# One hybrid decoder layer: heads interleaved with their up-projections, small work one tile later, the output halves reordered

## The chip, the core and the metric

The kernel runs on one core of a Trainium2 chip. The metric is the device time of one execution in microseconds (us); of several runs the median counts. Before the change three runs took 1225.09, 1226.62 and 1227.04 us: median 1226.62.

The engines are TensorE (PE in the profile; its weight loads are PEld), VectorE (DVE), ScalarE (ACT), GpSimd (POOL) and SyncE (SP), which here only issues DMAs. Each engine runs its own instructions strictly in the order of the program; between engines, semaphores hold an instruction back until its operands are there.

## What is computed

One decoder layer on 256 tokens of width 2048, in float32. One input projection feeds two groups of heads: an RWKV-7 mixer (16 heads of 64, a recurrence over the tokens) and a latent attention (8 heads of 128, with a rotary part). Both outputs are joined and projected back, and then comes a gated MLP with a short convolution. Cut to what matters here:

```python
h = rms_norm(x, attn_norm_g)
proj = h @ w_in                                  # 2048 x 4512
shifted = token_shift(proj[..., :RWKV_SHIFT_DIM], rwkv_mu)
h_r, h_k, h_v, h_w, h_a, h_g = _split(shifted, IN_SPLITS[:6])
c_q, c_kv, k_pe = _split(proj[..., RWKV_SHIFT_DIM:], IN_SPLITS[6:])
# rwkv7_mixer: per token  sa = state @ a_t
#   state = state * w_t + sa b_t + v_t k_t ;  y_t = state @ r_t
# then group norm, bonus, gate:  y = (gn(y) + bonus) * g
y_rwkv = rwkv7_mixer(h_r, h_k, h_v, h_w, h_a, h_g, ...)
# mla_mixer: q = rms_norm(c_q) @ w_uq ; k, v = rms_norm(c_kv) @ w_ukv
#   p = softmax(causal(q_nope k_nope + rope(q_pe) rope(k_pe))) ; out = p v
y_mla = mla_mixer(c_q, c_kv, k_pe, positions, ...)
x = x + concatenate([y_rwkv, y_mla]) @ w_out
x = x + conv_glu_ffn(rms_norm(x, ffn_norm_g), ...)
return rms_norm(x, final_norm_g)
```

## The kernel before, in words

**Products.** Weights come in pieces of 128x1024 floats (512 KB). `piece` (L123 to L130) loads one into `raw`, ScalarE makes the rounded half `hi`, VectorE the rest `lo = raw - hi`; three buffers each. `prod_b` (L156 for hi, L159 for lo) multiplies pieces with the stacked hi and lo halves of the activations into a PSUM tile `mm`; `prod_a` (L176 to L178) does the same with weights as the moving side. There are three `mm` buffers. `joined` (ScalarE L164, VectorE L165 and L166) reads the two halves of such a tile, adds and scales them; only then is its buffer free.

**Input tiles.** `in_tile(i)` does one tile of 128 columns of the input projection from two pieces. Small work that hangs behind a tile is put into a list, `pend`, and run by `flush`, which stands between the two pieces of the next `in_tile`. In this list are the key norms, the chunk products `gram`, the bonus and the solve.

**The solve.** The recurrence is done in four chunks of 64 tokens. `gram` makes each chunk's matrices `G` and stores their diagonal blocks to `dL` in device memory (16 stores). `solve` loads them as `Lp`, one row per system (L556), multiplies by the scales `Mp` on VectorE (L560), and runs 31 elimination steps on VectorE (`tm` L564, `Tq` L566). The inverse goes back by memory, is completed on TensorE (`pR` L609, `pT` L622), and stands in `TT`.

**The recurrence.** `chunk(c)` works in two halves of the heads. For each: `px` from the state `ST` and `UV`; VectorE makes `XB` (L669); `px` again from `XB` and `TT`; `UV` is copied by VectorE and ScalarE (L675); `pS` and `py` follow from `UV`, and VectorE updates `ST` (L688, L689). All TensorE rows of it carry L658, and all its PSUM tiles come from a pool `ch` of three.

**Attention.** `latent` makes the two normalized latents `cl`. `up_b` makes the up-projections: `wuq` tiles into `qn`, `wuk` tiles into `kn`, two tiles for each of two heads to a side, four times. `wuv` makes `vm`. For each head `scores(h)` fills `psc` (pool `at` of two) and does the softmax in `pexp` on VectorE and ScalarE; `attend(h)` transposes it (`ptp`), multiplies by `vm` (`po`) and writes `yhi[1]` and `ylo[1]`. `group_norm(w)` normalizes the recurrence's output `yt[w]` on VectorE (L700 to L722), multiplies by the gate (`pgate`), transposes (`pyT`), and writes `yhi[0]` and `ylo[0]`.

**Output.** `w_out` is done in two halves of its rows (half 0 takes the recurrence's output, half 1 that of attention) and four blocks of columns; `x1` collects the sums.

**What sets the order.** The program text gives priorities; a scheduler then fixes each engine's order of instructions when the kernel is built. So a block that is written earlier can still run late, and the order on each engine is what counts.

Of the kernel before, what the change touches and what calls it, by code (L numbers as in the profile page):

```python
# [54 lines left out]
def hybrid_layer(ctx: ExitStack, tc: tile.TileContext, a: dict, out: bass.AP):  # L55
    nc = tc.nc
# [15 lines left out]
    def s4(dt=F32, n="s4"):  # L72
        return sb.tile([P, 1024], dt, tag="s4", name=nm(n), bufs=NS4)

    def sv(n):
        return sb.tile([P, 1024], F32, tag="sv", name=nm(n), bufs=3)
# [67 lines left out]
    last_w, last_lo = [None], [None]  # L144
    pend = []

    def flush():
        while pend:
            pend.pop(0)()

# [29 lines left out]
    def in_tile(i, pf=mm):  # L182
        acc = pf()
        for h in range(2):
            prod_b(acc, piece(a["win"][i, h]), x_hl, h * 8, 8, h == 0, h == 1)
            if h == 0:
                flush()
        return acc

    def rsqrt(src, scale, eps, w, eng=None, part=None):  # L190
# [118 lines left out]
    with tc.manual_schedule(engines={mybir.EngineType.SP}):  # L309
        for g in range(4):  # L310
            xsplit(g)
            if g == 0:
                nc.scalar.dma_start(cst, a["cst"])
            if g == 2:
                rope_tables()
            if g % 2 == 0:
                for i in range(2):
                    pcs[i, g // 2] = piece(a["win"][wt0[i], g // 2])
            for i in range(2):
                hl = tuple(u[:, (g % 2) * 512:(g % 2 + 1) * 512] for u in pcs[i, g // 2])  # L320
                prod_b(acc0[i], hl, x_hl, g * 4, 4, g == 0, g == 3)
        for h in range(2):
            prod_b(acc0[2], piece(a["win"][26, h]), x_hl, h * 8, 8, h == 0, h == 1)
        sums(0)
        kacc[0] = in_tile(1)
        dve0 = last_lo[0]
        sums(1)
        kacc[1] = in_tile(2, ch)
        lora = s4(n="lora")
        nc.sync.dma_start(lora, a["lora"])  # L330

# [102 lines left out]
    for p in range(8):  # L434
        pp, g = p // 2, p % 2
        for q in range(4):
            if DP[q] == p:
                decay(q)
        acc = kacc[p] if p in kacc else in_tile(1 + p)
        k = shifted(acc, 1 + p)  # L440
        kc = k.rearrange("p (c t) -> p c t", t=64)
        sq = t1("ksq")
        S.activation(sq, k, AF.Square, scale=vv("kk", p))

        def key_ss(p=p, sq=sq):
            for w in range(2):
                PE.matmul(ssP[:, w * 16 + p * 2:w * 16 + p * 2 + 2], sq[:, w * P:(w + 1) * P], blk2,
                          start=True, stop=True)

        pend.append(key_ss)  # L450
        V.scalar_tensor_tensor(AR[pp][:, g, :, 0, 1:64], kc[:, :, 1:64], nkk[:, p:p + 1],
                               AR[pp][:, g, :, 1, 0:63], ALU.mult, ALU.mult)
        V.tensor_scalar(AR[pp][:, g, :, 0, 0:1], kc[:, :, 0:1], nkk[:, p:p + 1], None, ALU.mult)
        V.tensor_tensor(kv_(pp, g), kc, kv_(pp, g), ALU.mult)
        V.scalar_tensor_tensor(bv_(pp, g), kc, hkk[:, p:p + 1], bv_(pp, g), ALU.mult, ALU.mult)
# [17 lines left out]
        for pb in range(4):  # L473
            V.tensor_copy(Mp[pb * 32:(pb + 1) * 32, :], pmt[0:32, pb * 32:(pb + 1) * 32])

    pend.append(key_norms)


    BKt = []
# [1 line left out]
    dL = dr.tile([P, 32, 32], F32, name="dL")  # L481
# [3 lines left out]
    for p in range(8):  # L485
        pp, g = p // 2, p % 2
        acc = in_tile(9 + p)
        if p == 0:
            pend.append(key_norms_p)
        r = shifted(acc, 9 + p)  # L490
        rc = r.rearrange("p (c t) -> p c t", t=64)
        V.tensor_tensor(AR[pp][:, g, :, 1, :], rc, AR[pp][:, g, :, 1, :], ALU.mult)
        pr = t1("pr")
        V.tensor_tensor(pr.rearrange("p (c t) -> p c t", c=4), kv_(pp, g), AR[pp][:, g, :, 1, :], ALU.mult)

        def bonus(p=p, pr=pr):
            for w in range(2):
                PE.matmul(boP[:, w * 16 + p * 2:w * 16 + p * 2 + 2], pr[:, w * P:(w + 1) * P], brk[:, p, :],
                          start=True, stop=True)

        def gram(p=p, pp=pp):
            hf = p // 4
            e0 = (pp % 2) * 2
            for c in range(4):
                if pp % 2 == 0:
                    G1[c].append(s4(n="G1").rearrange("p (e t) -> p e t", e=8))
            for w in range(2):
                pg = [ch("pg") for _ in range(2)]
                for r in range(2):
                    for gg in range(2):  # L510
                        o = (r * 2 + gg) * P
                        for h in range(2):
                            hs = slice(h * 64, h * 64 + 64)
                            PE.matmul(pg[h][:, o:o + P], BK[pp][hs, gg, w * 2 + r, :, :],  # L514
                                      AR[pp][hs, gg, w * 2 + r, :, :], start=o == 0, stop=True,
                                      skip_group_check=True)
                for h in range(2):
                    for r in range(2):
                        V.tensor_tensor(G1[w * 2 + r][hf][:, h * 4 + e0:h * 4 + e0 + 2, :],
                                        pg[h][:, r * T:(r + 1) * T].rearrange("p (q t) -> p q t", q=2),  # L520
                                        gmask.unsqueeze(1).broadcast_to([P, 2, P]), ALU.mult)
            if pp % 2 == 1:
                for c in range(4):
                    for b in range(2):
                        r0 = 64 + b * 32
                        for h in range(2):
                            nc.sync.dma_start(dLv[b, c, :, h, hf * 4:hf * 4 + 4, :],
                                              G1[c][hf][r0:r0 + 32, h * 4:h * 4 + 4, b * 32:(b + 1) * 32])
            for c in range(3):
                if pp == 0:  # L530
                    BKt.append(s4(n="BKt").rearrange("p (a t) -> p a t", a=8))
                pt = ch("pt")
                for gg in range(2):
                    PE.transpose(pt[:, gg * P:(gg + 1) * P],
                                 BK[pp][:, gg, c, :, :].rearrange("p s t -> p (s t)"), ident)
                S.copy(BKt[c][:, pp * 2:pp * 2 + 2, :], pt[:, 0:T].rearrange("p (a t) -> p a t", a=2))

        pend.append(bonus)
        if g == 1:
            pend.append(gram)  # L540

    def bonus_rows():
        for r in range(2):
            V.tensor_copy(bon[:, r * 32:r * 32 + 32], boP[r * 64:r * 64 + 64, 0:32])

    pend.append(bonus_rows)


    TT = con([P, 32, 64], "TT")
    T11 = []  # L550

    def solve():
        Lp = sv("Lp").rearrange("p (i t) -> p i t", i=32)
        Tq = sv("Tq").rearrange("p (s t) -> p s t", s=32)
        tm = t1("tm")
        nc.sync.dma_start(Lp, dL)  # L556
        nc.gpsimd.memset(Tq, 0.0)
        nc.gpsimd.memset(Tq.rearrange("p s t -> p (s t)")[:, 0:1024:33], 1.0)
        nc.gpsimd.memset(TT, 0.0)
# [1 line left out]
        for i in range(31):  # L561
            n, m = i + 1, 31 - i
# [17 lines left out]
                k0 = h * 64 + b * 32  # L580
                nc.sync.dma_start(TT[k0:k0 + 32, :, b * 32:(b + 1) * 32], dT[k0:k0 + 32].rearrange("q s t -> s q t"))

    pend.append(solve)


    UV = [s4(n="UV").rearrange("p (e t) -> p e t", e=8) for _ in range(4)]
# [179 lines left out]

    latent(0, "qg", SC)
    latent(1, "kvg", 1.0)
    flush()
    qr = s4(n="qr").rearrange("p (h t) -> p h t", h=4)  # L770
    qs = sv("qs").rearrange("p (h t) -> p h t", h=4)
    qn, kn = a8("qn", F32), a8("kn", F32)
# [5 lines left out]
    def up_b(src, i, x, dsts):  # L778
        pcs = piece(src[i])
        for j in range(2):  # L780
            acc = mm()
            prod_b(acc, (pcs[0][:, j * 512:(j + 1) * 512], pcs[1][:, j * 512:(j + 1) * 512]),
                   lambda k: cl[x][k // 2][:, k % 2, :, :], 0, 4, True, True)
            joined(dsts[j], acc, rrB[x])
# [5 lines left out]
    V.tensor_tensor(qr, qr, cosR.unsqueeze(1).broadcast_to([P, 4, T]), ALU.mult)  # L790
    V.tensor_tensor(qs, qs, sinR.unsqueeze(1).broadcast_to([P, 4, T]), ALU.mult)
    V.tensor_tensor(qr, qr, qs, ALU.add)
    for i in range(4):
        up_b(a["wuq"], i, 0, [qn[:, i * 2 + j, :] for j in range(2)])
    for i in range(4):
        up_b(a["wuk"], i, 1, [kn[:, i * 2 + j, :] for j in range(2)])
    g2a = s4(n="g2a")
    g2b = s4(n="g2b")
    gnwb = [s4(n=n) for n in ("gnw", "gnb")]
# [5 lines left out]
    yhi = [[s4(F32R, "yhi").rearrange("p (k t) -> p k t", k=4) for _ in range(2)], a8("yhi")]  # L805
    ylo = [[s4(F32R, "ylo").rearrange("p (k t) -> p k t", k=4) for _ in range(2)], a8("ylo")]

    group_norm(0)
    for cc in range(2):
        accs = [mm() for _ in range(2)]  # L810
        for i in range(2):
# [2 lines left out]
                   i * 2, 2, i == 0, i == 1)  # L814
        for tb in range(2):
            S.activation(vm[tb][:, cc * 512:(cc + 1) * 512], accs[tb], AF.Copy, scale=rrs[1][:, tb:tb + 1])

    group_norm(1)

    soft = {}  # L820

# [33 lines left out]
        S.copy(yhi[1][:, h, :], po)  # L855
        V.tensor_tensor(ylo[1][:, h, :], po, yhi[1][:, h, :].bitcast(F32), ALU.subtract)

    for h in range(8):
        scores(h)
        if h > 0:  # L860
            attend(h - 1)
    attend(7)


# [7 lines left out]

    ssf = st("ssf", 8)
    zs = [hl4("z") for _ in range(4)]
    for half in (0, 1):
        for c in range(4):
            accs = [mm() for _ in range(2)]
            for i in range(4):
                if half == 0 and i == 2:
                    load_x1(c)  # L880
                prod_a(accs, piece(a["wout"][half, c, i]), lambda k: y_hl(yhi, half, k),
                       lambda k: y_hl(ylo, half, k), i * 2, 2, i == 0, i == 3)
            for tb in range(2):
                V.tensor_tensor(x1[c][:, tb, :], x1[c][:, tb, :], accs[tb], ALU.add)
            if half == 1:
                for tb in range(2):
                    scr = sb.tile([P, 512], F32, tag="xs", name=nm("scr"), bufs=2)
                    S.activation(scr, x1[c][:, tb, :], AF.Square, accum_out=ssf[:, tb * 4 + c:tb * 4 + c + 1])
# [39 lines left out]
    for blk, nf in enumerate((24, 20)):  # L928
        hh = [s4(F32R, "hh").rearrange("p (k t) -> p k t", k=4) for _ in range(nf // 4)]
        hl = [s4(F32R, "hl").rearrange("p (k t) -> p k t", k=4) for _ in range(nf // 4)]  # L930
        for fi in range(nf):
            f = f0 + fi
# [133 lines left out]
```

## Time and profile before

| | |
|---|---|
| median of three runs | 1226.62 us |
| the profiled execution | 1224.32 us |
| its span from first to last instruction | 1222.5 us |
| TensorE busy | 1186.5 us, 97% |
| VectorE busy | 837.9 us, 69% |
| ScalarE busy | 599.7 us, 49% |
| granted TensorE clock, mean | 0.986 |
| stages: input tiles, recurrence, heads, output, MLP | the MLP begins near 487 us and runs to the end |

In the rows that follow, a row of the timeline is: start, length, engine, line, operation, output <- inputs, shapes, count, and in brackets the idle time ahead of it on that engine with what ended it. A row of a group ends with busy us, mean ns of one | idle before. A row of waits is: who waited <- for whom: us in all, how often, the longest.

### The profile page before, as it was taken

The page shows a single profiled execution, that of the slowest core. Times are in us where ns is not written, and L with a number is a line of the kernel's source. Part 1 is how long each engine was busy: PE and PEld are TensorE (multiplying, and loading weights), DVE is VectorE, ACT ScalarE, POOL GpSimd, SP SyncE. Part 2 cuts the span into 40 slices and gives each one's busy share as a digit, 9 for nine tenths or more (in the row PEclk, how much of TensorE's full clock was granted, in tenths as well). Part 3 has the DMA queues.
Part 4 walks back from the last instruction along what each step waited for, and adds up shares of the span by engine and source line. Part 5 has one row for each costly group of instructions (what it writes and reads, how often), then busy time and mean ns, then how long its engine had stood idle before and what let it go on. Part 6 is the DMA issues. An engine that isn't in the chain of part 4 may idle for free.

```text
span 1222.5 us, 18434 instructions
## 1 busy us (share of the span) xinstructions
PE 1186.5 (97%) x6993; PEld 1001.6 (82%) x6993; DVE 837.9 (69%) x1359; ACT 599.7 (49%) x939; POOL 60.4 (5%) x202
## 2 busy tenths in 40 slices
PE   7989979999989999999999999999999999999996
PEld 5878868888847888888888888888888888888885
DVE  6898659868985656777777676454577777766563
ACT  6684425635334455555555554333455555554442
POOL 3400100002120001000000000000000000000000
PEclk9989999999999999999999999999999999999998
DMA  8735544744513555655555555666655555566662
GB/s 298 207 116 157 145 147 135 204 141 143 166 64 104 177 174 172 201 188 181 186 187 190 189 185 179 195 190 194 203 182 188 189 186 185 183 223 205 208 209 85
DMA packets 71017, 215.82 MB, mean 177 GB/s; under 512 B 17616, under 2 KB 17872, under 8 KB 70928
## 3 DMA queue, kind: packets, MB, share of 16 engines
q1 hardware_dynamic: 69776, 211.84, 53.9%
q10 hardware_dynamic: 768, 2.05, 0.6%
q8 instruction: 55, 0.90, 0.3%
q0 software_dynamic: 384, 0.75, 0.2%
q14 instruction: 34, 0.28, 0.1%
HBM read 210.48 MB, written 3.41 MB: 175 GB/s over the span
## 4 chain that ended last, share of the span: by engine, by line
PE 90%; DVE 3%; DMA 2%; ACT 2%; issue 1%; POOL 1%; SPq 0%; ACTq 0%; DVEq 0%; POOLq 0%
PE mm L156 38%; PE mm L159 19%; PE mm L177 9%; PE mm L178 9%; PE mm L176 9%; PE pg L514 1%; DMA raw<-in_win 1%; DVE lo L130 1%; ACT hi L129 1%; PE px L658 1%; DMA rp<-in_pos 0%; DMA Lp<-dL 0%; PE psc L834 0%; PE py L658 0%; PE psc L832 0%
## 5 line engine op out<-in xcount | busy, mean ns | idle before, releaser
L130 DVE TENSOR_TENSOR lo<-raw,hi 128x1024 fp32r<-128x1024 f32 x376 | 460.5, 1225 | 294.1 <-ACT hi L129 288.1
L129 ACT CAST hi<-raw 128x1024 fp32r<-128x1024 f32 x376 | 395.1, 1051 | 478.7 <-issue 259.7
L156 PE MATMUL mm<-z,hi 128*128 128x512 f32 x1408 | 356.9, 395 | 0.0
L156 PEld LDWEIGHTS mm<-z,hi 128*128 128x128 f32 x1408 | 253.3, 188 | 48.8
L159 PEld LDWEIGHTS mm<-z,lo 128*128 128x128 f32 x1408 | 192.8, 188 | 15.4
L159 PE MATMUL mm<-z,lo 128*128 128x256 f32 x1408 | 197.7, 282 | 0.0
L156 PE MATMUL mm<-x,hi 128*128 128x512 f32 x528 | 147.2, 415 | 15.7 <-DVE rp L249 8.2
L177 PE MATMUL mm<-lo,hh 128*128 128x512 f32 x336 | 130.7, 389 | 0.0
L178 PE MATMUL mm<-hi,hl 128*128 128x512 f32 x336 | 130.7, 389 | 0.0
L156 PEld LDWEIGHTS mm<-x,hi 128*128 128x128 f32 x528 | 98.7, 198 | 35.6 <-ACT hi L129 8.2
L176 PE MATMUL mm<-hi,hh 128*128 128x512 f32 x336 | 119.7, 389 | 0.0
L159 PEld LDWEIGHTS mm<-x,lo 128*128 128x128 f32 x528 | 75.3, 192 | 8.8 <-DVE lo L130 1.5
L159 PE MATMUL mm<-x,lo 128*128 128x256 f32 x528 | 81.3, 290 | 0.7 <-DVE lo L130 0.7
L176 PEld LDWEIGHTS mm<-hi,hh 128*128 128x128 f32 x336 | 63.1, 188 | 13.1
L177 PEld LDWEIGHTS mm<-lo,hh 128*128 128x128 f32 x336 | 63.1, 188 | 13.0
L178 PEld LDWEIGHTS mm<-hi,hl 128*128 128x128 f32 x336 | 63.1, 188 | 13.0
L177 PE MATMUL mm<-lo,yhi 128*128 128x512 f32 x128 | 51.4, 402 | 0.0
L178 PE MATMUL mm<-hi,ylo 128*128 128x512 f32 x128 | 50.6, 396 | 0.0
L176 PE MATMUL mm<-hi,yhi 128*128 128x512 f32 x128 | 49.1, 398 | 0.0
L940 POOL MEMSET gt<- 128x2 f32 x44 | 4.3, 99 | 587.2 <-DVE hl L952 570.0
L177 PEld LDWEIGHTS mm<-lo,yhi 128*128 128x128 f32 x128 | 24.1, 188 | 6.1 <-DVE lo L130 0.6
L176 PEld LDWEIGHTS mm<-hi,yhi 128*128 128x128 f32 x128 | 24.2, 189 | 5.2
(287 smaller groups left out, 1126.4 us busy)
## 6 DMA issues: line engine op xcount, KB each, us to landing
raw<-in_wgu SPq DMA_DIRECT2D x176, 512.0 KB, 3.3
raw<-in_wdn SPq DMA_DIRECT2D x88, 512.0 KB, 4.2
raw<-in_win SPq DMA_DIRECT2D x70, 512.0 KB, 3.7
raw<-in_wout SPq DMA_DIRECT2D x32, 512.0 KB, 3.5
raw<-in_wuq SPq DMA_DIRECT2D x6, 512.0 KB, 3.3
xraw<-in_xT SPq DMA_DIRECT2D x4, 512.0 KB, 6.1
xt<-in_x SPq DMA_DIRECT2D x4, 512.0 KB, 6.5
raw<-in_wuk SPq DMA_DIRECT2D x4, 512.0 KB, 3.3
```

The lines of the kernel that those rows point to most:

```text
L129: S.copy(hi, raw)
L130: last_lo[0] = V.tensor_tensor(lo, raw, hi.bitcast(F32), ALU.subtract).ins
L156: PE.matmul(acc, hi[:, j * P:(j + 1) * P], act(kt0 + j), start=first and j == 0, stop=False, skip_group_check=True)
L159: PE.matmul(acc[:, :T], lo[:, j * P:(j + 1) * P], act(kt0 + j)[:, 0, :], start=False, stop=last and j == n - 1, skip_group_check=True)
L176: PE.matmul(accs[tb], ah, wh, start=first and j == 0, stop=False)
L177: PE.matmul(accs[tb], ah, wl, start=False, stop=False)
L178: PE.matmul(accs[tb], al, wh, start=False, stop=last and j == n - 1)
L514: PE.matmul(pg[h][:, o:o + P], BK[pp][hs, gg, w * 2 + r, :, :], AR[pp][hs, gg, w * 2 + r, :, :], start=o == 0, stop=True, skip_group_check ...
L658: PE.matmul(dst[HS[h], a_ * 64:(a_ + 1) * 64], lhsT, rhs, start=n == 0 and a_ == 0, stop=True, skip_group_check=True)
L940: nc.gpsimd.memset(gt[:, 0:2], 0.0)
```

## The change

1. The rotary tables are written after the third input tile and not inside the loop over x.
2. `flush` stands behind the second piece of an input tile. Each entry of `pend` has a number; an entry with 1 is left for the next `flush`. Only the solve has 1; its load is an entry of its own with 0.
3. The `wuq` and `wuk` tiles are written between the heads: two heads' tiles, then the scores of these two heads and the output of the head before. `group_norm(0)` and `group_norm(1)` stand behind the first and the second pair.
4. `w_out` runs half 1 first. The loads of `x1` go with the first half that runs, the squares and transposes with the last.

```diff
-    def flush():
-        while pend:
-            pend.pop(0)()
+    def flush(every=False):
+        now = [f for n, f in pend if n == 0 or every]
+        pend[:] = [(n - 1, f) for n, f in pend if n > 0 and not every]
+        for f in now:
+            f()
...
             prod_b(acc, piece(a["win"][i, h]), x_hl, h * 8, 8, h == 0, h == 1)
-            if h == 0:
-                flush()
+        flush()
         return acc
...
-            if g == 2:
-                rope_tables()
...
     kacc[1] = in_tile(2, ch)
+    rope_tables()
...
+    def solve_load():
+        Lps.append(sv("Lp").rearrange("p (i t) -> p i t", i=32))
+        nc.sync.dma_start(Lps[0], dL)
+
     def solve():
-        Lp = sv("Lp").rearrange("p (i t) -> p i t", i=32)
+        Lp = Lps[0]
...
-        nc.sync.dma_start(Lp, dL)
...
-    pend.append(solve)
+    pend.append((0, solve_load))
+    pend.append((1, solve))
...
-    for i in range(4):
-        up_b(a["wuq"], i, 0, [qn[:, i * 2 + j, :] for j in range(2)])
-    for i in range(4):
-        up_b(a["wuk"], i, 1, [kn[:, i * 2 + j, :] for j in range(2)])
...
-    group_norm(0)
...
-    group_norm(1)
...
-    for h in range(8):
-        scores(h)
-        if h > 0:
-            attend(h - 1)
+    for i in range(4):
+        up_b(a["wuq"], i, 0, [qn[:, i * 2 + j, :] for j in range(2)])
+        up_b(a["wuk"], i, 1, [kn[:, i * 2 + j, :] for j in range(2)])
+        for h in range(2 * i, 2 * i + 2):
+            scores(h)
+            if h > 0:
+                attend(h - 1)
+        if i < 2:
+            group_norm(i)
     attend(7)
...
-    for half in (0, 1):
+    for half in (1, 0):
         for c in range(4):
...
-                if half == 0 and i == 2:
+                if half == 1 and i == 2:
                     load_x1(c)
...
-            if half == 1:
+            if half == 0:
```

The orders that come of it, at three places. Line numbers after the change are some 3 to 7 higher than before. First VectorE where the solve begins, before the change; `lo` rows are splits of weight pieces, `h` with `mm_1653` is the join of input tile 17:

```order
L130 TENSOR_TENSOR lo_1992<-raw_1989,hi_1991 128x1024
L130 TENSOR_TENSOR lo_2032<-raw_2029,hi_2031 128x1024
L560 TENSOR_TENSOR Lp_1736<-Lp_1736,Mp 128x1024
L564 TENSOR_TENSOR tm_1738<-Tq_1737,Lp_1736 128x31
L566 TENSOR_TENSOR Tq_1737<-Tq_1737,tm_1738 128x31
L165 TENSOR_TENSOR h_1843<-mm_1653,h_1843 128x256
```

The same place afterwards; `h_1896` with `mm_1768` is the join of tile 18:

```order
L130 TENSOR_TENSOR lo_2032<-raw_2029,hi_2031 128x1024
L130 TENSOR_TENSOR lo_2054<-raw_2051,hi_2053 128x1024
L566 TENSOR_TENSOR Lp_1758<-Lp_1758,Mp 128x1024
L130 TENSOR_TENSOR lo_2085<-raw_2082,hi_2084 128x1024
L570 TENSOR_TENSOR tm_1814<-Tq_1813,Lp_1758 128x31
L168 TENSOR_TENSOR h_1896<-mm_1768,h_1896 128x256
```

The join of tile 17 has moved ahead of the chunk matrices `G`; behind `Lp` now stands the join of tile 18, and one more split on either side of `Lp`.

On SP around the load, before the change, from the last stores of `dL`:

```order
L527 DMA dL<-G_1512 32x4x32 x3
L123 DMA raw_2051<-in_win 128x1024
L123 DMA raw_2082<-in_win 128x1024
L556 DMA Lp_1736<-dL 128x1024
L123 DMA raw_2104<-in_win 128x1024
```

And afterwards:

```order
L123 DMA raw_2051<-in_win 128x1024
L528 DMA dL<-G_1531 32x4x32 x4
L528 DMA dL<-G_1532 32x4x32 x4
L528 DMA dL<-G_1533 32x4x32 x4
L528 DMA dL<-G_1534 32x4x32 x4
L123 DMA raw_2082<-in_win 128x1024
L557 DMA Lp_1758<-dL 128x1024
```

The piece `raw_2051` went from behind the stores to ahead of them.

Last, TensorE in chunk 2 of the recurrence, before the change; `mm_3606` to `mm_3636` are up-projection tiles, and four such tiles more stand just ahead of these rows:

```order
L658 MATMUL px_2617<-XB_2405,TT 64x64 x8
L156 MATMUL mm_3606<-cl_3085,hi_3590 128x512 x2
L156 MATMUL mm_3606<-cl_3086,hi_3590 128x512 x2
L159 MATMUL mm_3606<-cl_3085,lo_3591 128x256 x2
L159 MATMUL mm_3606<-cl_3086,lo_3591 128x256 x2
L156 MATMUL mm_3624<-cl_3085,hi_3620 128x512 x2
L156 MATMUL mm_3624<-cl_3086,hi_3620 128x512 x2
```

The same place afterwards:

```order
L665 MATMUL px_2617<-XB_2405,TT 64x64 x8
L665 MATMUL pS_2647<-UV_1647,BKt_1238 64x64
L665 MATMUL py_2618<-ST_2401,AR_488 64x64 x4
L665 MATMUL py_2618<-ST_2401,AR_489 64x64 x4
L665 MATMUL py_2618<-UV_1647,G_1198 64x64
L665 MATMUL pS_2647<-UV_1647,BKt_1238 64x64 x7
L665 MATMUL py_2618<-UV_1647,G_1198 64x64 x7
L665 MATMUL px_2678<-ST_2402,AR_490 64x64 x4
```

From `pS_2586` to the last rows of `px_2787`, 36 rows, TensorE now has recurrence products alone; the up-projection tiles come behind them, among the heads' scores.

On VectorE, inside that stretch, these rows stand between the `UV` copy and the state update:

```order
L682 COPY UV_1647<-px_2678 64x4x64
L797 TENSOR_TENSOR qr_3335<-qr_3335,cosR 128x1024
L798 TENSOR_TENSOR qs_3336<-qs_3336,sinR 128x1024
L799 TENSOR_TENSOR qr_3335<-qr_3335,qs_3336 128x1024
L695 TENSOR_TENSOR ST_2402<-pS_2708,ST_2402 64x4x64 x2
```

The three rotary products of the queries stand ahead of the update of `ST_2402`, which the next `px` reads.

More of the change, by code (lines that the diff above doesn't have):

```diff
@@ L448, in key_ss @@
                           start=True, stop=True)
-        pend.append(key_ss)
+        pend.append((0, key_ss))
         V.scalar_tensor_tensor(AR[pp][:, g, :, 0, 1:64], kc[:, :, 1:64], nkk[:, p:p + 1],
@@ L474, in key_norms_p @@
             V.tensor_copy(Mp[pb * 32:(pb + 1) * 32, :], pmt[0:32, pb * 32:(pb + 1) * 32])
-    pend.append(key_norms)
+    pend.append((0, key_norms))
     BKt = []
@@ L488, in hybrid_layer @@
         if p == 0:
-            pend.append(key_norms_p)
+            pend.append((0, key_norms_p))
         r = shifted(acc, 9 + p)
@@ L536, in gram @@
                 S.copy(BKt[c][:, pp * 2:pp * 2 + 2, :], pt[:, 0:T].rearrange("p (a t) -> p a t", a=2))
-        pend.append(bonus)
+        pend.append((0, bonus))
         if g == 1:
-            pend.append(gram)
+            pend.append((0, gram))
     def bonus_rows():
@@ L544, in bonus_rows @@
             V.tensor_copy(bon[:, r * 32:r * 32 + 32], boP[r * 64:r * 64 + 64, 0:32])
-    pend.append(bonus_rows)
+    pend.append((0, bonus_rows))
     TT = con([P, 32, 64], "TT")
     T11 = []
+    Lps = []
+    def solve_load():
+        Lps.append(sv("Lp").rearrange("p (i t) -> p i t", i=32))
+        nc.sync.dma_start(Lps[0], dL)
     def solve():
-        Lp = sv("Lp").rearrange("p (i t) -> p i t", i=32)
+        Lp = Lps[0]
         Tq = sv("Tq").rearrange("p (s t) -> p s t", s=32)
         tm = t1("tm")
-        nc.sync.dma_start(Lp, dL)
         nc.gpsimd.memset(Tq, 0.0)
@@ L768, in hybrid_layer @@
     latent(1, "kvg", 1.0)
-    flush()
+    flush(True)
     qr = s4(n="qr").rearrange("p (h t) -> p h t", h=4)
```

## The prediction, made before the changed kernel had run

> **What bounds the kernel now.** I read the share of each engine on the page, then the chain that ended last, then what TensorE waited for.
>
> ```profile
> span 1222.5 us, 18434 instructions
> PE 1186.5 (97%) x6993; PEld 1001.6 (82%) x6993; DVE 837.9 (69%) x1359; ACT 599.7 (49%) x939; POOL 60.4 (5%) x202
> PE 90%; DVE 3%; DMA 2%; ACT 2%; issue 1%; POOL 1%; SPq 0%; ACTq 0%; DVEq 0%; POOLq 0%
> PE mm L156 <- DVE rp L249: 8.2, 1, 8.2
> PE mm L156 <- DVE h L165: 7.5, 2, 7.2
> PE ssP L447 <- ACT ksq L443: 3.1, 1, 3.1
> PE psc L827 <- ACT pexp L838: 2.9, 2, 1.6
> PE py L658 <- DVE UV L675: 1.3, 1, 1.3
> ```
>
> TensorE is busy 97% and carries 90% of the chain. The change neither adds nor removes a matrix product, so it can win only time in which TensorE waits or runs at a lowered clock, and lose by making such time. The profiled run took 1224.32 us, 2.3 below the median 1226.62; I sum against 1224.32 and then carry the difference over to the median.
>
> **Rotary tables and the later flush in the early tiles: 0.** On every engine the rows before tile 17 stand in the same order before and after, the table code included. So the start wait of 8.2 and the 3.1 at `ssP` stay. Were the 8.2 to move after all, the bounds are -8.2 and +8.2; I take 0, because no queue differs there.
>
> **The solve: -2.9.** This is the 7.2 wait.
>
> ```profile
> 157.08 2.03 PE L156 MATMUL mm<-x,hi 128*128 128x512 f32 x8
> 159.91 1.56 PE L156 MATMUL mm<-x,hi 128*128 128x512 f32 x6
> 176.47 0.33 SPq L556 DMA_DIRECT2D Lp<-dL  x1
> 182.05 1.23 DVE L560 TENSOR_TENSOR Lp<-Lp,Mp 128x1024 f32<-128x1024 f32 x1 [3.95 <-DMA Lp<-dL]
> 183.71 0.42 DVE L165 TENSOR_TENSOR h<-mm,h 128x256 f32<-128x256 f32 x1
> 184.18 3.78 PE L156 MATMUL mm<-x,hi 128*128 128x512 f32 x8 [7.25 <-DVE h L165]
> ```
>
> SP issues the load of `Lp` at 176.47 and VectorE stands idle 3.95 for it until 182.05. Behind it on VectorE is the join of a finished tile, and that join frees the one PSUM buffer that the next tile needs: TensorE waits 7.25. Its next eight products then take 3.78, where the same eight at 157.08 take about 1.9, so the low clock adds 1.9.
>
> Afterwards the load, the first tile's join and the solve stand one tile later: the join behind `Lp` is that of tile 18. One piece is 159.91 - 157.08 = 2.83, a tile 5.65, so TensorE arrives at 176.93 + 5.65 = 182.6. `Lp` also starts later, since one more weight piece now stands ahead of the 16 `dL` stores on SP: I estimate its issue at 178.5, and with the 5.6 from issue to use it lands at 184.1. Then come `Lp` 1.23, one `lo` split 1.22 that now stands behind it, and the join 0.42: 187.0, so the wait is 4.4 and the low clock stays. Gain 7.25 - 4.4 = 2.9; bounds -9.2 (no wait, no low clock) and +1.
>
> **The recurrence without cover: +7.0 of waiting.** This is the step that costs most. The sixteen up-projection tiles used to stand between the steps of the chunk recurrence; now they stand beside the heads. From the state product of chunk 1's second half to the last `px` of chunk 3, TensorE has 36 rows and not one large product.
>
> ```profile
> 324.46 0.69 PE L658 MATMUL px<-XB,TT 128*64 128x64 f32 x16
> 325.07 0.50 PE L177 MATMUL mm<-lo,cl 128*128 128x512 f32 x1
> 327.79 0.27 PE L658 MATMUL pS<-UV,BKt 128*64 128x64 f32 x1
> 329.24 0.69 PE L658 MATMUL px<-ST,AR 128*64 128x64 f32 x16
> 330.32 0.48 PE L834 MATMUL psc<-kpe,qr 64*128 64x128 f32 x2
> L669 DVE TENSOR_TENSOR XB<-px,mtok 64x256 f32<-64x256 f32 x16 | 6.7, 422 | 0.2
> L675 DVE COPY UV<-px 64x256 f32<-64x256 f32 x8 | 3.3, 418 | 0.8 <-PE px L658 0.6
> L688 DVE TENSOR_TENSOR ST<-pS,ST 64x256 f32<-64x256 f32 x8 | 3.4, 419 | 0.1
> L790 DVE TENSOR_TENSOR qr<-qr,cosR 128x1024 f32<-128x1024 f32 x1 | 1.2, 1219 | 0.0
> 301.00 0.37 ACT L675 COPY UV<-px 64x256 f32<-64x256 f32 x1 [0.29 <-DVE UV L675]
> ```
>
> A step's `pS` and `py` block begins at 327.79 and runs until the `px` at 329.24: 1.45. The first `px` block takes 330.32 - 329.24 = 1.08, its `XB` products 325.07 - 324.46 = 0.61. Between them VectorE does four `ST` instructions (4 x 0.42) and two `XB` (2 x 0.42), then one `UV` copy of 0.42, and ScalarE another of 0.37 behind it. From the start of one block: pS and py end at 1.45, ST at 3.2, XB at 4.1, the `XB` products at 4.7, UV at 5.5, where the next block may start. So 5.5 us pass for 1.45 + 1.08 + 0.61 = 3.1 us of work. In the third step three rotary instructions of 1.22 stand ahead of ST on VectorE (3.7 more). Over the stretch I get 18 us for 11 us of work: 7.0 idle. The bounds are 0 and 9. Ahead of the stretch I count some five waits of about 1 us in the same chain; part of them is in the old time too, so I take +1.5, between 0 and 5.
>
> **The clock in that stretch: +3.** These are the windows of ten microseconds from 330 to 380, with busy time of TensorE, weight loads, VectorE, ScalarE and GpSimd, then the granted clock.
>
> ```profile
> 330.00:340.00 10.00, 9.85 (x141) 6.35 (x137) 8.10 (x12) 2.00 (x6) 5.13 (x14) 1.00 0.25 79
> 340.00:350.00 10.00, 8.49 (x35) 3.71 (x34) 8.74 (x11) 4.18 (x9) 0.00 (x0) 0.83 0.00 1
> 350.00:360.00 10.00, 10.00 (x41) 6.65 (x39) 6.88 (x9) 4.72 (x10) 6.76 (x14) 1.00 0.25 75
> 360.00:370.00 10.00, 7.12 (x23) 3.94 (x22) 8.49 (x19) 1.58 (x6) 0.00 (x0) 0.77 0.22 84
> 370.00:380.00 10.00, 10.00 (x47) 8.01 (x47) 6.92 (x13) 7.21 (x16) 0.00 (x0) 0.89 0.23 77
> ```
>
> The clock fell to 0.83 and 0.77 where TensorE waited 1.3 to 1.6 us at a time. In the uncovered stretch it will wait up to 2.2 us at a time, over and over, so two such falls, of 1.5 each, are my estimate; 0 and 5 are the bounds. [...]
>
> **The heads: -5.2.** In the rows from 340 to 380 TensorE lost 1.51 + 2.88 = 4.4 us idle and, by the clock, 0.17 + 0.23 + 0.11 of ten each, 5.1 us: 9.5, where group norm and softmax stood uncovered. All of it I let go. In its place come new waits, and for these I walked VectorE against TensorE from the end of the recurrence to the transposes of the first normalized block.
>
> ```profile
> 314.54 1.08 PE L156 MATMUL mm<-cl,hi 128*128 128x512 f32 x4
> 316.02 0.27 PE L658 MATMUL pS<-UV,BKt 128*64 128x64 f32 x1
> 378.04 0.38 PE L832 MATMUL psc<-kn,qn 128*128 128x128 f32 x2
> 380.02 0.50 PE L177 MATMUL mm<-lo,yhi 128*128 128x512 f32 x1
> 347.30 1.02 PE L720 MATMUL pgate<-g2a,sg 128*128 128x512 f32 x2
> 349.31 1.13 PE L720 MATMUL pgate<-g2a,sg 128*128 128x512 f32 x2
> L130 DVE TENSOR_TENSOR lo<-raw,hi 128x1024 fp32r<-128x1024 f32 x31 | 38.0, 1224 | 13.1 <-ACT hi L129 12.9
> L165 DVE TENSOR_TENSOR qn<-mm,qn 128x256 f32<-128x256 f32 x8 | 3.3, 418 | 0.0
> L708 DVE TENSOR_TENSOR yt<-yt,ry 128x1024 f32<-128x1024 f32 x2 | 2.5, 1225 | 3.9 <-POOL ry L210 3.9
> 343.83 1.21 DVE L700 TENSOR_REDUCE gmu<-yt 128x16 f32<-128x1024 f32 x1
> 344.96 0.68 DVE L722 TENSOR_TENSOR yt<-yt,pgate 128x512 f32<-128x512 f32 x1
> ```
>
> TensorE: sixteen up tiles at 1.5 (314.54 to 316.02), six heads' scores at 2.15 (1.98 from 378.04 to 380.02, and 0.17 for the mask), two gates at 2.0, and 7.2 of rest (twelve products of the value tiles 2.8, the recurrence's last blocks 2.1, one head's transposes and output 0.9, six output products 1.4): 24 + 12.9 + 4.1 + 7.2 = 48. VectorE can start on the first scores 14.8 after that point (2.8 + 2.1 + six tiles 9 + half a score 0.9). From there to the gated block it has 62 instructions: five `lo` splits 6.1, twenty-one joins of 0.42, 8.8, twenty softmax instructions of 0.16 to 0.42, 6.0, fifteen of group norm 15.1, one `ylo` 0.4. That is 36.4, less 0.08 each where one starts before the other has ended (1.21 long, the next one 1.13 behind): 31.4, so it is through at 46, 2 us before TensorE. What remains are PSUM buffers that `pyT` and the softmax transposes share (three), by my walk 2.1, 1.0 and 1.2 us. Sum -9.5 + 4.3 = -5.2; bounds -9.5 and +5.
>
> **Output halves reordered: 0 by itself.** The same 32 pieces run; what it changes, that half 1 has only three accumulators to run beside the heads, is in the 1.2 above. The second half's residual adds and transposes keep their place behind the last pieces. It costs 5 at most, if the last heads lie bare.
>
> **Sum.** -2.9 + 7.0 + 1.5 + 3 - 5.2 = +3.4: 1227.7 against the profiled 1224.32, and 1230 against the median.
>
> **The rivals.**
> - **VectorE becomes the bound beside the heads.** For it: it was 8.7 busy of ten at 340, and its margin is 2 us of 46. Without the overlap of 0.08 it comes at 51, and the second block loses as much again, 4, with two falls of the clock: about +8, so 1238. It decides if the gated block is ready after TensorE's transposes come up. Chance 0.15.
> - [...] Chance 0.18.
> - **The solve's load arrives in time, and the kernel gets faster.** If `Lp` lands by 179.5, the join is done before TensorE arrives at 182.6: the whole 9.2 goes in place of 2.9, 6.3 more, so 1223.7. It decides at 3 us or less between landing and arrival; against it stands the start of the load, some 178. Chance 0.25, which also holds smaller waits in the recurrence.
> - **The change doesn't do what it says** for the tables and the early flush: there the rows are the same, and that is in the sum already.
>
> **How the numbers follow.** The forecast, 1230 with 1226 to 1235 as its own range, has 0.42. Under 0.2% (2.4 us) a measurement of this kernel can't tell a difference from none. The forecast puts 0.30 above that bound and 0.12 within; the first rival 0.15 above; the second 0.10 within, 0.04 on either side; the third 0.25 below. So faster 0.29, same 0.22, slower 0.49. The range goes from 1218, past the third rival with the clock holding, to 1241, past the first.
>
> **What would show it.** In the new profile: TensorE's longest wait on a join near 180 should be 4.4 and not 7.2 or 0; a stretch near 295 to 313 with only `px`, `py` and `pS` should have TensorE idle for about 7 us, its releasers XB, UV and ST, and a clock below 1; the waits of `psc` on `pexp` should be gone, and `pyT` should wait under 2. The forecast is wrong if the recurrence finds its operands ready, or if VectorE is late at the gated block.

## The result, and the profile after

Over 20 runs each the changed kernel took 1228.32 us (median) and the kernel before 1224.97. The ratio is 1.0022, with a 95% interval of 1.0012 to 1.0032: slower by 2.7 us of 1225, where 3.4 was forecast. (The medians differ by 3.35; differences below go by the ratios, which use every run.) The profiled run of the changed kernel took 1226.27 us.

The page after, the chain, and TensorE's longest waits:

```profile
span 1224.5 us, 18446 instructions
PE 1186.1 (97%) x6993; PEld 1001.4 (82%) x6993; DVE 836.4 (68%) x1359; ACT 599.7 (49%) x939; POOL 57.5 (5%) x202
PE 90%; DVE 4%; DMA 2%; ACT 2%; issue 1%; SPq 0%; ACTq 0%; POOL 0%; DVEq 0%; POOLq 0%
PE mm L159 <- DVE rp L251: 8.3, 1, 8.3
PE mm L159 <- DVE h L168: 3.9, 2, 3.1
PE px L665 <- DVE XB L676: 3.7, 3, 1.4
PE pyT L733 <- DVE yt L729: 3.0, 1, 3.0
PE ssP L448 <- ACT ksq L444: 2.4, 1, 2.4
```

The page hardly differs; the waits do. The 7.2 at the solve became 3.1, and new waits stand in the recurrence (`px` on `XB`) and beside the heads (`pyT` on `yt`). Three windows show where: the solve, the recurrence, the heads. Columns: busy time of TensorE, weight loads, VectorE, ScalarE and GpSimd, then granted clock, DMA share, GB/s. Before:

```profile
160.00:200.00 40.00, 32.75 (x193) 27.82 (x192) 26.52 (x59) 15.63 (x28) 0.39 (x4) 0.91 0.45 138
255.00:335.00 80.00, 78.56 (x1008) 67.56 (x1004) 69.56 (x131) 35.10 (x67) 9.44 (x23) 1.00 0.45 143
335.00:400.00 65.00, 60.46 (x289) 40.25 (x288) 45.31 (x82) 27.70 (x65) 9.45 (x24) 0.92 0.25 83
```

And after:

```profile
160.00:200.00 40.00, 36.95 (x231) 31.67 (x230) 28.72 (x62) 20.52 (x36) 0.49 (x5) 1.00 0.52 154
255.00:335.00 80.00, 73.95 (x1025) 62.05 (x1025) 58.55 (x118) 35.06 (x74) 5.14 (x18) 0.98 0.36 115
335.00:400.00 65.00, 58.02 (x243) 39.87 (x242) 48.87 (x89) 24.79 (x59) 10.34 (x28) 0.92 0.22 73
```

TensorE idles 36.95 - 32.75 = 4.2 less at the solve, 78.56 - 73.95 = 4.6 more in the recurrence, and 60.46 - 58.02 = 2.4 more beside the heads. The clock rose by 0.09 in the first window, fell by 0.02 in the second and stayed at 0.92 in the third.

**The solve.** SP's issue of the load, VectorE's start on it, and TensorE's end of the wait, after the change:

```profile
177.75 0.34 SPq L557 DMA_DIRECT2D Lp<-dL  x1
181.08 1.22 DVE L566 TENSOR_TENSOR Lp<-Lp,Mp 128x1024 f32<-128x1024 f32 x1 [1.62 <-DMA Lp<-dL]
183.93 2.13 PE L159 MATMUL mm<-x,hi 128*128 128x512 f32 x8 [3.05 <-DVE h L168]
```

The issue at 177.75 is near the 178.5 of the prediction, but the load took 3.3 and not 5.6 us. TensorE came sooner too, at 183.93 - 3.05 = 180.9 and not at 182.6. So the wait is 3.05 and not 4.4; and the eight products behind it took 2.13, so in this profile the lowered clock is gone as well. It need not be: in two of the later runs with these edits (the rotation left out, eight tiles as cover with the old halves), with waits of 3.1 and 3.0 on the join, the mean clock from 160 to 200 was 0.96, where it is 1.00 here.

**The recurrence.** The first row of the bare stretch and the waits in it, VectorE's first rotary product in it, and four windows of five microseconds:

```profile
290.34 0.27 PE L665 MATMUL pS<-UV,BKt 128*64 128x64 f32 x1
294.33 0.69 PE L665 MATMUL px<-XB,TT 128*64 128x64 f32 x16 [1.40 <-DVE XB L676]
295.54 0.33 PE L665 MATMUL pS<-UV,BKt 128*64 128x64 f32 x2 [0.52 <-DVE UV L682]
299.53 0.69 PE L665 MATMUL px<-XB,TT 128*64 128x64 f32 x16 [1.34 <-DVE XB L676]
300.74 0.33 PE L665 MATMUL pS<-UV,BKt 128*64 128x64 f32 x2 [0.52 <-DVE UV L682]
305.26 0.69 PE L665 MATMUL py<-ST,AR 128*64 128x64 f32 x16 [0.52 <-DVE ST L695]
300.71 1.23 DVE L797 TENSOR_TENSOR qr<-qr,cosR 128x1024 f32<-128x1024 f32 x1
290.00:295.00 5.00, 3.60 (x98) 3.11 (x97) 2.66 (x7) 1.10 (x3) 0.00 (x0) 1.00 0.85 284
295.00:300.00 5.00, 3.14 (x98) 2.99 (x96) 2.94 (x7) 1.10 (x3) 0.00 (x0) 1.00 0.72 223
300.00:305.00 5.00, 4.22 (x88) 3.90 (x84) 4.64 (x6) 2.93 (x6) 0.00 (x0) 0.67 0.06 18
305.00:310.00 5.00, 4.60 (x73) 3.92 (x74) 3.06 (x8) 0.69 (x2) 0.00 (x0) 0.99 0.01 3
```

From one `pS` block to the next, 295.54 to 300.74, pass 5.2 us (5.5 was worked out). The whole stretch, from 290.34 to the large product at 307.92, took 17.6 us (18 was worked out). TensorE idles 4.4 of the 20 us of the windows, and the clock fell once.

**The heads.** TensorE's first large product after the stretch, its last product ahead of the transposes of the normalized block, and these transposes; VectorE's first row of the scores and its two longest waits for scores, and three windows, the first of them from that row to the gated block:

```profile
307.92 0.51 PE L179 MATMUL mm<-hi,cl 128*128 128x512 f32 x1
357.11 0.39 PE L181 MATMUL mm<-hi,ylo 128*128 128x512 f32 x1
360.52 1.97 PE L733 MATMUL pyT<-cst,yt 128*128 128x128 f32 x8 [3.01 <-DVE yt L729]
324.52 0.28 DVE L837 TENSOR_REDUCE mx<-psc 128x1 f32<-128x128 f32 x1
329.06 0.29 DVE L837 TENSOR_REDUCE mx<-psc 128x1 f32<-128x128 f32 x1 [1.22 <-PE psc L834]
344.15 0.29 DVE L837 TENSOR_REDUCE mx<-psc 128x1 f32<-128x128 f32 x1 [1.84 <-PE psc L834]
324.52:360.45 35.93, 31.58 (x145) 21.36 (x143) 31.58 (x63) 15.11 (x35) 5.26 (x14) 0.99 0.27 88
350.00:360.00 10.00, 7.50 (x35) 5.12 (x33) 10.00 (x22) 2.40 (x4) 0.00 (x0) 0.98 0.28 86
360.00:370.00 10.00, 8.92 (x28) 6.84 (x28) 8.44 (x13) 4.12 (x12) 5.07 (x14) 0.50 0.38 125
```

In the first window VectorE is busy 31.6 of 35.9 us and idle for 4.4. From 350 to 360 it is busy 10.00 of ten while TensorE waits for it, and the ten microseconds after that run at half the clock.

### The profile page after: what moved, and what is told of

Same layout as the page of the kernel before. It is cut to its first block, busy times and chain, and to the rows that moved or that the text cites. A ratio compares the mean times of both kernels' runs of the same rounds, so it can differ in the third digit from the quotient of the medians.

```text
span 1224.5 us, 18446 instructions
## 1 busy us (share of the span) xinstructions
PE 1186.1 (97%) x6993; PEld 1001.4 (82%) x6993; DVE 836.4 (68%) x1359; ACT 599.7 (49%) x939; POOL 57.5 (5%) x202
## 3 DMA queue, kind: packets, MB, share of 16 engines
q1 hardware_dynamic: 69776, 211.84, 52.5%
HBM read 210.48 MB, written 3.41 MB: 175 GB/s over the span
## 4 chain that ended last, share of the span: by engine, by line
PE 90%; DVE 4%; DMA 2%; ACT 2%; issue 1%; SPq 0%; ACTq 0%; POOL 0%; DVEq 0%; POOLq 0%
PE mm L159 37%; PE mm L162 19%; PE mm L179 9%; PE mm L181 9%; PE mm L180 9%; PE pg L515 1%; DMA raw<-in_win 1%; DVE lo L130 1%; PE px L665 1%; PE psc L834 1%; ACT hi L129 0%; DMA rp<-in_pos 0%; DMA xt<-in_x 0%; PE psc L832 0%; PE py L665 0%
## 5 line engine op out<-in xcount | busy, mean ns | idle before, releaser
L159 PE MATMUL mm<-x,hi 128*128 128x512 f32 x528 | 144.4, 409 | 12.1 <-DVE rp L251 8.3
L159 PEld LDWEIGHTS mm<-x,hi 128*128 128x128 f32 x528 | 96.6, 194 | 31.4 <-ACT hi L129 8.3
L181 PEld LDWEIGHTS mm<-hi,ylo 128*128 128x128 f32 x128 | 23.9, 188 | 5.8 <-issue 0.8
```

Source lines behind the costliest of these rows:

```text
L159: PE.matmul(acc, hi[:, j * P:(j + 1) * P], act(kt0 + j), start=first and j == 0, stop=False, skip_group_check=True)
L181: PE.matmul(accs[tb], al, wh, start=False, stop=last and j == n - 1)
```

## The experiments

All ratios are against the kernel before, run on the same chip; in brackets the 95% interval. One thousandth is 1.2 us. Two variants are compared through their ratios. The intervals reach 1.2 to 2.1 us to either side, so a difference of two variants is uncertain by some 2 us.

### Each part alone

The kernel before with the solve edits only (point 2 of the change; the diff is that of `flush`, `solve_load` and `solve`, shown above):

> The later flush and the split solve alone; everything else as before. Theory A (each stage keeps its own loss): the two traces put the gain between 160 and 200 us at 5.7 us (wait 7.25 to 3.05, and no lowered clock), so this kernel is 5.7 faster than before, ratio near 0.995. Theory B (the gain is lost again further on, because the solve ends one tile later and the first product with its result waits): 0 to 2 us faster.

Measured: 0.9956 [0.9943, 0.9970], 5.4 us faster. Theory A. Nearly all of the gain holds to the end. Its windows at recurrence and heads show what is given back:

```profile
255.00:335.00 80.00, 75.26 (x984) 64.13 (x982) 66.89 (x125) 32.07 (x62) 11.40 (x32) 0.96 0.42 134
335.00:400.00 65.00, 62.66 (x296) 42.77 (x297) 44.38 (x82) 28.74 (x67) 6.76 (x14) 0.89 0.24 82
```

Over both windows TensorE idles 4.74 + 2.34 = 7.1 us, where it idled 1.44 + 4.54 = 6.0 before, at a clock 0.03 to 0.04 lower. So with a later solve a little of the cover is lost by itself. It also moves idle time across 335 us, and so the two windows are added wherever kernels are compared: 6.05 + 6.98 = 13.0 in the changed kernel.

The interleaving alone:

```diff
-        up_b(a["wuq"], i, 0, ...)      # before the value tiles
-    group_norm(0)
-    group_norm(1)
+    for i in range(4):                 # the loop over pairs, as in the change
```

> The interleaving of heads and up-projections alone, with group norm behind the first two pairs; solve and output order as before. Theory A (the recurrence without cover is what costs): TensorE again idle for about 7 us in the rows with px, py and pS alone, 8 us of loss there, and about 8 us slower than before, ratio near 1.0065. Theory B (the order of the halves is what costs; the interleaving by itself wins the waits of the heads): 0 to 4 us faster than before.

Measured: 1.0030 [1.0020, 1.0041], 3.7 us slower: the direction of theory A and about half its size. TensorE's longest new waits are again `px` on `XB` (2.8 in all) and `pyT` on `yt` (2.7).

The order of the halves alone:

```diff
-    for half in (0, 1):
+    for half in (1, 0):
```

> The order of the output halves alone. Theory A as the prediction had it (nothing by itself but small waits): 0 to 2 us slower. Theory B (half 0 was the work that covered heads 1 to 7; with half 1 first only two accumulators' products can stand beside the heads, and each head's chain of transposes, softmax and output lies bare): 8 to 15 us slower, with waits of po and ptp rows between 360 and 420 us.

Measured: 1.0068 [1.0054, 1.0082], 8.3 us slower. That is the size of theory B, and the prediction's 0 for this part is refuted. The waits, though, are not where theory B had them: `psc` waits for `pexp` 4.5 us in all, 3.9 at the longest, and `po` only 0.6.

Interleaving and halves together, solve as before:

> Interleaving and reversed halves together, solve as before; this is the changed kernel without the solve and table edits. Theory A (stages add up): the changed kernel's 3.4 over before, plus the 5.7 that the solve wins: 9 us slower, ratio near 1.0075. Theory B (the parts are not additive, the solve's later end is what bares the recurrence): no more than 4 us slower.

Measured: 1.0062 [1.0047, 1.0078], 7.6 us slower. Theory A's 1.0075 lies within the interval, theory B's 4 us does not. Against the changed kernel's 2.7 the solve edits are worth 4.9 in it. But interleaving and halves don't add: 3.7 + 8.3 would be 12.

### The changed kernel with one part undone

The old order of the halves in the changed kernel:

> The changed kernel with the output halves in the old order. Theory A (half 0 covers heads and softmax also beside interleaved tiles, as the two orders alone differ by 4 us with the old solve): 4 us faster than the changed kernel, 1 to 2 under before. Theory B (beside interleaved up-projections the order of halves no longer matters): within 1 us of the changed kernel.

Measured: 0.9993 [0.9981, 1.0005], 3.6 us faster than the changed kernel. Theory A: the reversed halves cost 3.6 even beside interleaved heads.

Without the interleaving, halves reversed:

> The changed kernel without the interleaving: solve and table edits and reversed halves. Theory A (the halves cost 8 us wherever the heads are not interleaved): the solve's 0.9956 and 8.3 us, ratio near 1.0024, as slow as the changed kernel. Theory B (the halves' cost was that run's lowered clock, 20 us of it, and goes with another phase): 3 us or more faster than the changed kernel.

Measured: 1.0039 [1.0027, 1.0051], slower than the forecast of theory A, 2 us slower than the changed kernel. Its first long wait beside the heads, and its window there:

```profile
354.76 0.32 PE L834 MATMUL psc<-cmb,idb 128*128 128x384 bf16 x1 [3.90 <-ACT pexp L845]
335.00:400.00 65.00, 58.55 (x264) 39.09 (x261) 37.60 (x76) 26.70 (x67) 7.04 (x14) 0.82 0.12 41
```

With half 1 first, the scores wait 3.90 for the softmax of the heads before, VectorE is idle for 27 of 65 us, and the clock over the whole window is 0.82, where the run with the solve edits alone had 0.89 and no wait of the scores over 1.2. That is a chain with little beside it: with half 0 first, products of finished recurrence output stood there (in the kernel before, `mm<-lo,yhi` at 380.02).

So with the solve edits in, the four kernels stand so (each against the kernel before):

| | halves (0, 1) | halves (1, 0) |
|---|---|---|
| up tiles ahead | 0.9956 | 1.0039 |
| up tiles between the heads | 0.9993 | 1.0022 |

Interleaving costs 4.5 us in the first column. There TensorE's idle time grows in the recurrence, from 4.74 to 7.42 (TensorE busy 72.58 of 80 us), but also beside the heads, from 2.34 to 3.92 (busy 61.08 of 65), so the lost cover is a part of the cost and not all of it. In the second column interleaving seems to win 2.1, but the two intervals overlap. The idle time beside the heads does not fall there (6.45 without, 6.98 with it); what rises is the clock, from 0.82 to 0.92.

### Is it the cover?

The changed kernel with half of the up-projection tiles, those of the first four heads, back ahead of the value tiles:

```diff
+    for i in range(2):
+        up_b(a["wuq"], i, 0, [qn[:, i * 2 + j, :] for j in range(2)])
+        up_b(a["wuk"], i, 1, [kn[:, i * 2 + j, :] for j in range(2)])
...
     for i in range(4):
-        up_b(a["wuq"], i, 0, ...)
-        up_b(a["wuk"], i, 1, ...)
+        if i > 1:
+            up_b(a["wuq"], i, 0, ...)
+            up_b(a["wuk"], i, 1, ...)
```

> The changed kernel with the up-projection tiles of the first two pairs of heads written where they were before, ahead of the value tiles; the other eight tiles stay between the heads. Theory A (cover decides in the recurrence): the loss from 255 to 335 us falls from 14.7 to about 11, 3 to 4 us faster than the changed kernel. Theory B (what lies bare is the last third, px_2678 to px_2787, and it stays bare): no faster, within 1 us.

Measured: 1218.59 us, 0.9941 [0.9929, 0.9953]: 7.2 under before and 9.9 under the changed kernel, well past what either theory gave. Its windows at recurrence and heads:

```profile
255.00:335.00 80.00, 76.58 (x1032) 64.33 (x1031) 64.27 (x125) 37.11 (x75) 8.37 (x21) 0.98 0.37 121
335.00:400.00 65.00, 59.33 (x270) 40.22 (x270) 48.43 (x88) 26.02 (x60) 9.28 (x26) 1.00 0.28 97
```

TensorE's idle time in the recurrence falls from 6.05 to 3.42, beside the heads from 6.98 to 5.67, 9.1 in place of 13.0, and beside the heads the clock is 1.00 in place of 0.92. So in the recurrence the cover decides: with eight tiles back it idles less even than with sixteen (4.74 in the run with the solve edits alone). But this is 2.6 of the 9.9 us. The larger part is won beside the heads, and most of that is the clock: 0.08 of 65 us is 5.2. It is no chance of one profile, since the mean clock was 0.991 to 0.994 in all five runs and 0.986 to 0.990 in the twenty of the changed kernel. Why the clock holds there is not shown. That fewer splits and joins compete with the group norm on VectorE is one thought, but VectorE was busy for 48.4 us in that window and for 48.9 in the changed kernel. (The 14.7 of the expectation is not the idle time of these rows; they give 6.05 idle and 1.6 for the clock.)

The same with the old order of halves:

> Eight up-projection tiles kept as cover, eight between the heads, and the output halves in the old order. Theory A (cover and the order of halves add up): the cover's 1218.6 less the 3 to 4 us that the old order gave beside interleaved tiles, 1215 us, ratio near 0.991. Theory B (with the recurrence covered the heads are no longer bare, and the order of halves does nothing): 1218 to 1219, ratio 0.994.

Measured: 1217.46 us, 0.9933 [0.9917, 0.9950]. Closer to theory B; the two intervals overlap, and these kernels can't be told apart. Its windows:

```profile
255.00:335.00 80.00, 76.59 (x1031) 64.44 (x1029) 64.57 (x126) 37.31 (x76) 8.74 (x21) 0.98 0.35 121
335.00:400.00 65.00, 61.69 (x279) 44.35 (x279) 48.90 (x87) 26.46 (x59) 8.92 (x25) 0.95 0.32 108
```

TensorE idles 3.41 + 3.31 = 6.7 us, though `pyT` waits 3.3 in this run; so that wait alone doesn't make the heads dear. Both kernels beat the changed kernel and the kernel before. They lie 1.8 and 2.8 us under the solve edits alone, but all these intervals overlap: that half the cover is better than all of it is likely and not shown.

### Smaller suspects

The rotary tables: the solve edits together with the tables' new place.

> The solve edits and the rotary tables' new place, nothing else. Theory A (the tables' place does not change any engine's order): the same as the solve edits alone, 1221.5, ratio 0.9956 within 0.0015. Theory B (the tables matter): off by 2 us or more. [...]

Measured: 0.9959 [0.9945, 0.9973] beside 0.9956 without: no difference, theory A.

The three rotary products in the bare stretch, first moved to GpSimd:

```diff
-    V.tensor_tensor(qr, qr, cosR..., ALU.mult)      # and the two rows behind it
+    nc.gpsimd.tensor_tensor(qr, qr, cosR..., ALU.mult)
```

> The changed kernel with the three rotary products of the queries given to GpSimd; TensorE's order is unchanged, VectorE's loses only these three rows. Theory A (they stand ahead of the state update in the uncovered stretch and hold the next px for 3.7 us): 3 to 4 us faster than the changed kernel, some 0 over before. Theory B (the stretch is bound by the steps' own chain of XB, UV and ST, or the heads give the time back): within 1 us of the changed kernel, 3 over before.

Measured: 1.0044 [1.0031, 1.0058], 2.7 us slower than the changed kernel. Neither theory; VectorE, GpSimd and TensorE in the stretch tell why:

```profile
293.14 0.88 DVE L695 TENSOR_TENSOR ST<-pS,ST 64x256 f32<-64x256 f32 x2 [1.52 <-PE pS L665]
294.05 4.25 DVE L696 TENSOR_TENSOR ST<-ST,PC 64x256 f32<-64x256 f32 x2
293.18 2.35 POOL L797 TENSOR_TENSOR qr<-qr,cosR 128x1024 f32<-128x1024 f32 x1 [4.13 <-PE pS L665]
295.50 2.51 POOL L798 TENSOR_TENSOR qs<-qs,sinR 128x1024 f32<-128x1024 f32 x1
298.09 2.42 POOL L799 TENSOR_TENSOR qr<-qr,qs 128x1024 f32<-128x1024 f32 x1
298.31 0.86 DVE L676 TENSOR_TENSOR XB<-px,mtok 64x256 f32<-64x256 f32 x2
299.22 1.12 PE L665 MATMUL px<-XB,TT 128*64 128x64 f32 x16 [4.79 <-DVE XB L676]
```

Two state products that take 0.85 elsewhere (at 304.00 in this run, with GpSimd idle) took 4.25 beside GpSimd's products, and TensorE waited 4.79 for what stood behind them. The run says nothing about the rotary products' own cost, so they were left out altogether (the queries are not rotated, and the scores lack that part):

> The changed kernel without the three rotary products of the queries (left out, so the scores lack the query's rotation); TensorE's order stays. Theory A (as the prediction had it: they hold the state update for 3.7 us in the bare stretch): 3.5 us faster than the changed kernel. Theory B (the next product waits 0.5 us only for the state, and the chain hides most): 0.5 to 2 us faster. GpSimd does nothing in this stretch, so the 4.25 us of one state product in the run with the rotation on GpSimd must be gone: 0.85 for two again.

Measured: 1.0011 [1.0001, 1.0020], 1.4 us faster than the changed kernel. The intervals overlap, so this can't be told from nothing; it fits theory B and speaks against the 3.5 of theory A. `px` waited 1.4 at the longest for `XB`, where it had waited 4.79 with the rotation on GpSimd. The rotary products hold the state update by 3.7 us, but `py` waited only 0.52 for the state in the changed kernel (the row at 305.26), since TensorE was still at work on the step before, at a clock of 0.67.

The second group norm one pair later:

```diff
-        if i < 2:
-            group_norm(i)
+        if i in (0, 2):
+            group_norm(i // 2)
```

> The changed kernel with the second group norm written behind the third pair of heads and not the second. Theory A (VectorE is late at the first gated block because the second block's first instructions, 2.6 us, stand ahead of it; the 3.0 us wait of pyT and the ten us of lowered clock behind it follow from that): 4 to 6 us faster than the changed kernel, about 2 under before. Theory B (another wait of the heads takes its place, since VectorE's work is only moved): within 1.5 us of the changed kernel.

Measured: 1.0053 [1.0035, 1.0070], 3.8 us slower than the changed kernel. Theory A falls, and theory B's 1.5 us is passed too. The longest wait of `pyT` became 2.0 only, and waits of 1.9 on a weight split and 1.9 on the state took its place. Why it came out slower than the changed kernel, and not the same, stays open. Its eight runs spread from 1228 to 1238, at mean clocks of 0.982 to 0.986, where the changed kernel had 0.986 to 0.990.

## Why the prediction was right in its total, and where its steps were not

**The total** was right: +3.4 forecast, +2.7 measured, in the range, slower. It was right by errors that cancel, which is luck: the solve won 2.0 more than its term, the recurrence lost some 5 less (4.6 idle and at most 1.6 of clock against 11.5), and the heads, with the output halves beside them, cost 7.6 more (2.4 lost against 5.2 won).

**The tables and the early flush, 0:** right. The start wait is 8.3 (8.2 before), and the run with the tables moved shows no difference. The wait at `ssP` is 2.4 in the profile after and 2.8 to 3.3 in those of the variants.

**The solve, -2.9:** the mechanism was right, the size too small. The term mis-sized is the load (3.3 us and not 5.6), of which TensorE's earlier arrival took a part back; and the low clock, which I had kept, went too in the profile after, though not in every later one. By the pair of kernels with and without it the part is worth 4.9, alone 5.4. Behind it stands the third rival's mechanism, half fulfilled: the load was early, though not by 179.5.

**The recurrence, +7.0 of waiting, +1.5 and +3 of clock:** the mechanism was right and shown: the same releasers `XB`, `UV` and `ST`, the same step length, and half the cover put back takes away 2.6 us of 6.05 idle. The size was too large. The length of the stretch was right, 17.6 us for 18, but I put TensorE's work in it at 11 us and it was busy for 13.2, a part of that at a lowered clock; so 4.4 were idle and not 7.0. The rotary products held the state update by the 3.7 that I had counted, but `py` waited only 0.52 for it. Idle time over the whole recurrence grew by 4.6, a part of it from the later solve. The clock fell once and not twice: 0.02 of 80 us is 1.6, at most, since TensorE also waited while it was low.

**The heads, -5.2:** wrong, and this is the step that failed. The old waits of the scores shrank from 2.9 to 1.4, where I had them gone. The step that failed is the overlap: I took VectorE to be through at 46, two microseconds before TensorE. The walk added up VectorE's work from the first score on as if it never waited again. The work was right, 31.6 us where 31.4 was worked out. But VectorE began 1.8 late (324.52, where 307.9 plus 14.8 gives 322.7), and then it was idle for 4.4 us, 1.22 and 1.84 of them in waits for scores. It was through 52.5 us after 307.9 and not 46. TensorE came at 357.5, 49.6 after it and not 48, and waited 3.01, and the clock fell for ten microseconds: the first rival's mechanism, to which I gave 0.15. In all the heads lost 2.4 us more idle time than before, at the same clock of 0.92; of the 9.5 that were to go, nothing was won.

**The halves, 0 by themselves:** wrong. They cost 8.3 alone and 3.6 in the changed kernel. I had noted that half 1 has only three accumulators beside the heads, and priced it at one wait of 1.2; what counts is that half 0's sixteen pieces, which need only the recurrence, no longer stand beside the heads. That this is the reason is read from the order of the products; no run moves these pieces alone.

**The clock.** I let two falls follow from waits of 2 us, an estimate from the rows at 340 and 360. One fall came, 0.67 from 300 to 305, behind waits of at most 1.4 us: neither two nor none. See the last section.

## What to carry to other kernels

Before large products are moved out from beside a chain of small dependent steps, count the chain's waits without them, and move only what the place they go to can use: here moving half of them was 7 to 10 us better than moving all, and moving none lay within the noise of half. Where two engines have nearly the same work in a stage, as TensorE and VectorE beside these heads, a margin of 2 in 48 us is none, since each wait of one for the other comes on top (4.4 us here). And which half of an output product runs first is a question of what it can stand beside.

## What the runs showed of the hardware

**The clock fell where the profile shows no idle time.** In the run with the solve edits alone TensorE is busy throughout these windows, 3.00 of 3.00 us in each, and yet the granted clock is 0.50 to 0.64. The profile models when a matmul ends, so short gaps between small products can't be ruled out; it shows no wait there. Ahead of them stand the solve's 32x32 products. Products, and windows with TensorE's busy time first and the clock third from last:

```profile
248.28 2.21 PE L617 MATMUL pR<-T,G 32*32 32x32 f32 x124
255.17 4.69 PE L630 MATMUL pT<-TT,RT 32*32 32x32 f32 x128
251.00:254.00 3.00, 3.00 (x13) 2.61 (x12) 2.78 (x5) 1.62 (x3) 0.00 (x0) 0.51 0.74 279
257.00:260.00 3.00, 3.00 (x77) 2.94 (x76) 1.47 (x3) 0.00 (x0) 0.00 (x0) 0.64 0.08 29
260.00:263.00 3.00, 3.00 (x25) 2.88 (x24) 2.11 (x4) 0.00 (x0) 0.00 (x0) 0.50 0.00 0
```

The run with the tables moved as well has the same order of instructions on TensorE, and there the first fall is missing and the second is shorter:

```profile
251.00:254.00 3.00, 3.00 (x19) 2.54 (x18) 2.88 (x6) 1.63 (x3) 0.00 (x0) 1.00 0.87 298
260.00:263.00 3.00, 3.00 (x11) 2.48 (x11) 1.64 (x2) 0.00 (x0) 0.00 (x0) 0.63 0.04 8
```

So with one order of instructions the clock fell in one run and not, or for a shorter time, in the other; what decides it was not shown. In the traces before and after the change, every fall, but for one at the very end of the kernel, is to 0.50 and lasts 3.4 us (from 249.3 and 341.5 before, from 250.5 and 301.7 after), 6.8 us (from 68.4, 181.1 and 365.4 before, from 66.1 after) or 10.2 us (from 359.7 after). The runs without and with the tables moved had 10.2 and 3.4 us of half clock from 248 to 266, and yet ratios of 0.9956 and 0.9959; so the parts above are judged by the times of many runs.

**VectorE was held up beside GpSimd.** Two products of VectorE with both operands in SBUF took 4.25 us in place of 0.85 (at 304.00 in the same run, and at 292.56 in the changed kernel) while GpSimd multiplied 128x1024 tiles; they ended at 298.30, just behind the second of these (298.01). Two with one operand in PSUM, at 293.14 and 298.31, took their usual 0.88 and 0.86 beside GpSimd's first and third product. GpSimd's own three took 2.35 to 2.51; what they take with VectorE at rest was not measured. Moving the rotation to an idle GpSimd was 2.7 us dearer than leaving it on VectorE.
